# Attention in a two-layer hybrid backbone: one product for two heads' prompt logits, and the maxima's transposes one tile later

## The chip, the cores and the metric

The kernel runs on one core of a Trainium2 chip. The metric is the device time of one execution in microseconds (us); smaller is better. The core's engines work from queues of their own, in the order in which the program was laid out at compile time: TensorE (PE, with its weight loads as PEld), VectorE (DVE), ScalarE (ACT), GpSimd (POOL) and SyncE (SP), which here issues nearly all transfers.

## The reference, cut to what matters

Two layers run over 128 prompt tokens and 1024 latent tokens. In each layer attention (8 heads of 64, 2 key/value heads), a gated convolution and a long convolution run side by side on parts of one projection; their outputs are joined, projected and added, and a convolutional feed-forward part follows. Prompt tokens attend only to the prompt's own keys; latent tokens attend to their own keys and to 128 cached ones.

```python
def _blocked_attention(q, k, v):          # q (B, Lq, H, d); k, v (B, Lk, KV, d)
    ...
    def one_block(qi):
        s = jnp.einsum('bqkgd,bskd->bkgqs', qi, k, preferred_element_type=jnp.float32) * scale
        p = jax.nn.softmax(s, axis=-1).astype(v.dtype)
        return jnp.einsum('bkgqs,bskd->bqkgd', p, v)
    ...

def _layer(x, cond, p, pos, ctx_kv):
    ...
    if pos is None:                       # prompt
        keys, vals = k, v
    else:                                 # latents
        q, k = _rope_2d(q, rows, cols), _rope_2d(k, rows, cols)
        keys = jnp.concatenate([k, ctx_kv[0].astype(k.dtype)], axis=1)
        vals = jnp.concatenate([v, ctx_kv[1].astype(v.dtype)], axis=1)
    attn_out = _blocked_attention(q, keys, vals)
    ...
```

## The kernel before

Each layer has four phases: phase1 (norm, projection of the input, the long convolution, the norm and rotation of q and k), phase2 (attention, the gated convolution's taps, and products for the modulation vectors), phase3 (output projection) and phase4 (feed-forward). The order of the instructions in each engine's queue is laid out at compile time by a planner: it simulates the program with its own costs and gives each engine, whenever it is free in that simulation, the ready instruction with the highest priority. Priority is the program's order, shifted by named offsets: `soon()` moves what is inside 100 instructions ahead (OUT_PRIO), and the taps are moved 300 back (TAPS_PRIO), so that they fill VectorE's gaps.

The latents' attention works on head pairs j = 0 to 3, in two halves of 512 queries. `attention` (line 1375) has 4 x 2 x 9 = 72 loop steps a layer. A step makes the logits of one block of 128 keys for two heads (tile st, in a single buffer), has ScalarE take the exponentials (tile p), and multiplies earlier p by the values (tile av). In each step it also calls `next` on the generator `maxes` of the next head pair and on each side generator: the prompt's attention, the convolution (six taps a step, then its later parts), and the modulation. After the 40th step the side generators are called three times a step.

The softmax's maximum over the keys must be known before st is formed. `maxes` (line 1329) computes the logits a first time, in the other orientation: for each block (512 queries of one head) four tiles of 128 queries, each of three products S of 384 keys, each followed by a maximum on VectorE (tile mx, line 1357). S has three PSUM buffers. After the fourth tile three small steps on VectorE (lines 1363 to 1365) form the negated maximum as two parts (tile nmx); TensorE transposes them (tile mxt, in the same three buffers), and ScalarE copies them into two spare rows of the query tile (line 1347), so that the product for st subtracts the maximum. These transposes are queued behind tile MX_LAG of the next block (`put`, line 1343); for the first two blocks of a layer (MX_NOW) at once; for the last block of a head pair at the end of the generator, one loop step later.

`prompt_attention` (line 1286) treats one head pair in two loop steps. The first loads q, and for each of the two heads forms a product of 64 rows (tile sp), takes the maximum (pnb, line 1306), negates it (line 1307), and takes the exponentials with their sums (pp). The second step scales by the sums' reciprocals (line 1313), transposes (ppt), copies (ppm) and multiplies by the values (avp). All PSUM tiles of the side generators, and the row sums of the latents, share one bank (pool pa, one buffer): each of its users must wait until the last reader of the one before is done.

Of the kernel before, what the change touches and what calls it, by code (L numbers as in the profile page):

```python
# [9 lines left out]
F32 = mybir.dt.float32  # L10
F32R = mybir.dt.float32r
AF = mybir.ActivationFunctionType
ALU = mybir.AluOpType
AX = mybir.AxisListType
# [114 lines left out]

MX_LAG = 1  # L130

# [5 lines left out]
class Kern:  # L137
# [1148 lines left out]
    def prompt_attention(self, l, kp):  # L1286
        nc = self.nc
        KP = []
        for g in range(2):
            t = kp.tile([128, 128], F32, tag=f"kp{g}", name="kpt")  # L1290
            for u in range(2):
                nc.sync.dma_start(t[64 * u : 64 * u + 64, :], self.kpD[64 * g : 64 * g + 64, :])
            KP.append(t)
        VP = kp.tile([128, 128], F32, tag="vp", name="vpt")
        nc.sync.dma_start(VP[:], self.vpD[:])
        for j in range(4):
# [3 lines left out]
            rs = self.small([128, 2], "prs")  # L1300
            for hd in range(2):
                r = slice(64 * hd, 64 * hd + 64)
                t = self.T("sp")
                self.mm(t[:, :128], qp[r, :128], KP[g][r, :], True, True)
                nb = self.small([128, 1], "pnb")
                nc.vector.tensor_reduce(nb[:], t[:, :128], op=ALU.max, axis=AX.X)
                nc.vector.tensor_scalar(nb[:], nb[:], -1.0, None, op0=ALU.mult)
                self.act(P[:, 128 * hd : 128 * hd + 128], t[:, :128], AF.Exp, bias=nb[:], accum_out=rs[:, hd : hd + 1])
            nc.vector.reciprocal(rs[:], rs[:])
            yield  # L1310
            for hd in range(2):
                p = P[:, 128 * hd : 128 * hd + 128]
                nc.vector.tensor_scalar(p, p, rs[:, hd : hd + 1], None, op0=ALU.mult)
            t = self.T("ppt")
# [14 lines left out]
    def maxes(self, j):  # L1329
# [19 lines left out]
        for half in range(2):  # L1349
            for a, b in Q:  # L1350
                m3 = self.small([128, 4, 3], "mx3")
                for k in range(4):
# [8 lines left out]
                    if k == 3:  # L1361
                        mx, n = self.small([128, 4], "mx"), self.small([128, 4, 2], "nmx", F32R)
                        nc.vector.tensor_reduce(mx[:], m3[:], op=ALU.max, axis=AX.X)
                        nc.vector.tensor_scalar(n[:, :, 0], mx[:], -1.0, None, op0=ALU.mult)
                        self.stt(n[:, :, 1], mx[:], -1.0, n[:, :, 0].bitcast(F32), ALU.mult, ALU.subtract)
                        tail = b, half, n
                        if MX_NOW(j, half):
                            put(*tail)
                            tail = None
# [514 lines left out]
```

## Time and profile before

| | us |
|---|---|
| median of 3 runs | 3329.2 (3327.6 to 3332.85) |
| profiled execution: its own time | 3328.34 |
| its span, first to last instruction | 3326.3 |
| TensorE busy | 3126.4 (94%) |
| VectorE busy | 2167.1 (65%) |
| ScalarE busy | 1188.7 (36%) |
| GpSimd busy | 400.8 (12%) |

Busy time is the time in which an engine had an instruction in work; a share of it is an average over phases with different limits. The granted clock is that of TensorE, as a share of its full 2.4 GHz: 0.50 is the lower level of 1.2 GHz. A row of the timeline gives start and duration in us, then the engine, the source line, the operation, and out<-in by the names of the tiles; in brackets stands the time that the engine had been idle before it, and what released it. All times are from the first instruction of the span. Times on GpSimd and ends of matmuls are rough.

### The profile page before, as it was taken

Reading aid. Unit: us, or ns where it says so; the run is one execution under the profiler, and the core shown is the slowest. Engines: PE = TensorE matmul, PEld = TensorE weight load, DVE = VectorE, ACT = ScalarE, POOL = GpSimd, SP = SyncE. Lnnn points to the kernel's source line nnn. Section 1 sums busy time; section 2 is a strip of 40 time slices with the busy share of each in tenths; the row PEclk is TensorE's granted clock in tenths of the full one; section 3 lists DMA queues with packets and bytes.
Section 4 is the critical chain, followed back from the end, with each engine's and each line's share of the span. In section 5 each row is a group of like instructions: output and inputs, shape, how many; then the busy total and the mean of one; then the engine's idle time right before and its main releaser. Section 6 shows DMA issues by size and latency. Waiting matters only on the chain. (4 is left out here: it accounts for less than half of the span.)

```text
span 3326.3 us, 44636 instructions
## 1 busy us (share of the span) xinstructions
PE 3126.4 (94%) x17330; PEld 2763.4 (83%) x17330; DVE 2167.1 (65%) x3556; ACT 1188.7 (36%) x1964; POOL 400.8 (12%) x328
## 2 busy tenths in 40 slices
PE   5999788999799999999998997799999999999997
PEld 3899733459799999999998995345799999999997
DVE  6888799655765544555567897987265455555556
ACT  3433333452352223333344333335243333333223
POOL 5200034221210000000010003322110000000002
PEclk8899878999899999999999997899999999999998
DMA  7565535544311111111113546341511111111112
GB/s 282 168 235 176 172 133 171 175 164 140 127 39 43 43 42 42 43 44 42 42 57 134 167 143 207 111 159 65 187 30 47 42 45 42 42 42 45 42 42 70
DMA packets 152326, 336.08 MB, mean 101 GB/s; under 512 B 21359, under 2 KB 57843, under 8 KB 145588
## 3 DMA queue, kind: packets, MB, share of 16 engines
q1 hardware_dynamic: 147412, 318.69, 29.7%
q0 software_dynamic: 4704, 14.55, 1.5%
q8 instruction: 137, 2.24, 0.3%
q14 instruction: 73, 0.60, 0.1%
HBM read 264.86 MB, written 68.31 MB: 100 GB/s over the span
## 5 line engine op out<-in xcount | busy, mean ns | idle before, releaser
L241 PE MATMUL up<-hl,whi 128*128 128x384 f32 (+1 forms) x2112 | 712.6, 338 | 4.9 <-DVE hl L227 3.2
L241 PE MATMUL up<-hh,whi 128*128 128x384 f32 (+1 forms) x2112 | 709.8, 337 | 3.6 <-ACT hh L212 2.7
L241 PE MATMUL up<-hh,wlo 128*128 128x384 f32 (+1 forms) x2112 | 711.6, 337 | 0.0
L215 DVE TENSOR_TENSOR wlo<-wraw,whi 128x512 fp32r<-128x512 f32 x362 | 253.0, 699 | 646.9 <-ACT whi L235 646.5
L235 ACT CAST whi<-wraw 128x512 fp32r<-128x512 f32 x362 | 223.7, 618 | 876.2 <-PE dn L241 358.2
L241 PEld LDWEIGHTS up<-hl,whi 128*128 128x128 f32 x2112 | 398.7, 189 | 7.1 <-DVE hl L227 4.9
L241 PEld LDWEIGHTS up<-hh,whi 128*128 128x128 f32 x2112 | 398.1, 189 | 4.3 <-ACT hh L212 3.1
L241 PEld LDWEIGHTS up<-hh,wlo 128*128 128x128 f32 x2112 | 398.6, 189 | 0.0
L227 DVE SCALAR_TENSOR_TENSOR xt<-dn,mod,xt 128x128 f32<-128x128 f32 (+2 forms) x704 | 332.1, 512 | 71.4 <-PE dn L241 71.1
L241 PE MATMUL dn<-gh,wlo 128*128 128x384 f32 (+1 forms) x1056 | 359.0, 340 | 0.0
L241 PE MATMUL dn<-gh,whi 128*128 128x384 f32 (+1 forms) x1056 | 358.1, 339 | 0.0
L241 PE MATMUL dn<-gl,whi 128*128 128x384 f32 (+1 forms) x1056 | 357.4, 338 | 0.0
L227 DVE SCALAR_TENSOR_TENSOR fu<-pd,vec,fu 128x1154 f32<-128x1154 f32 (+2 forms) x192 | 253.9, 1323 | 91.7 <-ACT fu L212 89.2
L241 PE MATMUL win<-hl,whi 128*128 128x384 f32 x768 | 264.5, 344 | 5.2 <-DVE hl L227 5.1
L241 PE MATMUL win<-hh,wlo 128*128 128x384 f32 x768 | 262.4, 343 | 3.2 <-DVE wlo L215 3.2
L241 PE MATMUL win<-hh,whi 128*128 128x384 f32 x768 | 262.2, 345 | 2.8 <-ACT hh L212 1.1
L215 POOL TENSOR_TENSOR acc<-acc,sq 128x384 f32<-128x384 f32 x51 | 55.1, 1090 | 1635.6 <-ACT sq L212 1634.5
L1678 ACT COPY pd<-up 128x384 f32<-128x384 f32 (+1 forms) x352 | 131.8, 401 | 239.6 <-PE up L241 239.6
L1357 DVE TENSOR_REDUCE mx<-S 128x1 f32<-128x384 f32 x384 | 196.0, 546 | 28.2 <-PE S L241 27.3
L212 ACT ACTIVATE p<-st 128x1024 f32<-128x1024 f32 x144 | 147.1, 1022 | 162.8 <-PE st L241 162.2
L241 PEld LDWEIGHTS dn<-gl,whi 128*128 128x128 f32 x1056 | 199.9, 189 | 0.0
L241 PEld LDWEIGHTS dn<-gh,whi 128*128 128x128 f32 x1056 | 199.7, 189 | 0.0
(293 smaller groups left out, 5092.8 us busy)
## 6 DMA issues: line engine op xcount, KB each, us to landing
wmod<-in_w_mod SPq DMA_DIRECT2D x48, 1024.0 KB
wraw<-in_w_up SPq DMA_DIRECT2D x176, 256.0 KB
wraw<-in_w_dn SPq DMA_DIRECT2D x88, 256.0 KB
wraw<-in_w_in SPq DMA_DIRECT2D x64, 256.0 KB
q<-qD SPq DMA_DIRECT2D x48, 256.0 KB
mh<-mixD SPq DMA_DIRECT2D x16, 576.0 KB
ml<-mixD SPq DMA_DIRECT2D x16, 576.0 KB
khD<-fK SPq DMA_DIRECT2D x16, 512.0 KB
```

What stands on the lines that cost most here:

```text
L212: return self.nc.scalar.activation(out, in_, f, **k)
L215: return (eng or self.nc.vector).tensor_tensor(out, a, b, op=op)
L227: return (eng or self.nc.vector).scalar_tensor_tensor(out, a, s, b, op0=op0, op1=op1)
L235: self.nc.scalar.copy(hi, src)
L241: self.nc.tensor.matmul(out, l, r, start=start, stop=stop)
L1357: nc.vector.tensor_reduce(m3[:, k, s : s + 1], S[:, :384], op=ALU.max, axis=AX.X)
L1678: self.nc.scalar.copy(p[:, u + o : v + o], t[:, u - a : v - a])
```

## The change

The prompt's keys lie in a tile of 128 rows and two column blocks for each key head: the keys' 64 rows stand in the upper half of the first block and in the lower half of the second one, the other halves are set to zero by GpSimd. One product of 128 rows and 256 columns then gives the logits of both heads. One maximum over a 3-D view, one negation, two exponentials and the scaling follow it, all moved ahead by `soon()`. A head pair now takes four loop steps in place of two: load q; product and softmax; nothing; transposes and values. In `maxes` the transposes are queued one tile later (MX_LAG 2), and the three small steps that feed them are moved ahead by `soon()`.

```diff
@@ -127,7 +127,7 @@
 
 ORDER = [([10, 11, 12, 13, 14, 15, 0, 4, 5, 1, 8, 6, 9, 7, 2, 3], 9), ([10, 11, 12, 13, 14, 15, 0, 4, 5, 1, 8, 6, 9, 7, 2, 3], 9)]
 
-MX_LAG = 1
+MX_LAG = 2
 
 
 def MX_NOW(j, half):
@@ -1287,9 +1287,11 @@
         nc = self.nc
         KP = []
         for g in range(2):
-            t = kp.tile([128, 128], F32, tag=f"kp{g}", name="kpt")
+
+            t = kp.tile([128, 2, 128], F32, tag=f"kp{g}", name="kpt")
             for u in range(2):
-                nc.sync.dma_start(t[64 * u : 64 * u + 64, :], self.kpD[64 * g : 64 * g + 64, :])
+                nc.gpsimd.memset(t[64 * u : 64 * u + 64, 1 - u, :], 0.0)
+                nc.sync.dma_start(t[64 * u : 64 * u + 64, u, :], self.kpD[64 * g : 64 * g + 64, :])
             KP.append(t)
         VP = kp.tile([128, 128], F32, tag="vp", name="vpt")
         nc.sync.dma_start(VP[:], self.vpD[:])
@@ -1298,19 +1300,22 @@
             qp, P = self.M("qp"), self.M("pp")
             nc.sync.dma_start(qp[:, :128], self.qpD[j])
             rs = self.small([128, 2], "prs")
-            for hd in range(2):
-                r = slice(64 * hd, 64 * hd + 64)
-                t = self.T("sp")
-                self.mm(t[:, :128], qp[r, :128], KP[g][r, :], True, True)
-                nb = self.small([128, 1], "pnb")
-                nc.vector.tensor_reduce(nb[:], t[:, :128], op=ALU.max, axis=AX.X)
+
+            yield
+            t = self.T("sp")
+            self.mm(t[:, :256], qp[:, :128], KP[g][:].rearrange("p a b -> p (a b)"), True, True)
+            with self.soon():
+                nb = self.small([128, 2], "pnb")
+                nc.vector.tensor_reduce(nb[:], t[:, :256].rearrange("p (a b) -> p a b", a=2), op=ALU.max, axis=AX.X)
                 nc.vector.tensor_scalar(nb[:], nb[:], -1.0, None, op0=ALU.mult)
-                self.act(P[:, 128 * hd : 128 * hd + 128], t[:, :128], AF.Exp, bias=nb[:], accum_out=rs[:, hd : hd + 1])
-            nc.vector.reciprocal(rs[:], rs[:])
-            yield
-            for hd in range(2):
-                p = P[:, 128 * hd : 128 * hd + 128]
-                nc.vector.tensor_scalar(p, p, rs[:, hd : hd + 1], None, op0=ALU.mult)
+                for hd in range(2):
+                    self.act(P[:, 128 * hd : 128 * hd + 128], t[:, 128 * hd : 128 * hd + 128], AF.Exp, bias=nb[:, hd : hd + 1], accum_out=rs[:, hd : hd + 1])
+                nc.vector.reciprocal(rs[:], rs[:])
+                for hd in range(2):
+                    p = P[:, 128 * hd : 128 * hd + 128]
+                    nc.vector.tensor_scalar(p, p, rs[:, hd : hd + 1], None, op0=ALU.mult)
+            yield
+            yield
             t = self.T("ppt")
             for hd in range(2):
                 self.tr(t[:, 128 * hd : 128 * hd + 128], P[:, 128 * hd : 128 * hd + 128])
@@ -1360,9 +1365,10 @@
                         tail = None
                     if k == 3:
                         mx, n = self.small([128, 4], "mx"), self.small([128, 4, 2], "nmx", F32R)
-                        nc.vector.tensor_reduce(mx[:], m3[:], op=ALU.max, axis=AX.X)
-                        nc.vector.tensor_scalar(n[:, :, 0], mx[:], -1.0, None, op0=ALU.mult)
-                        self.stt(n[:, :, 1], mx[:], -1.0, n[:, :, 0].bitcast(F32), ALU.mult, ALU.subtract)
+                        with self.soon():
+                            nc.vector.tensor_reduce(mx[:], m3[:], op=ALU.max, axis=AX.X)
+                            nc.vector.tensor_scalar(n[:, :, 0], mx[:], -1.0, None, op0=ALU.mult)
+                            self.stt(n[:, :, 1], mx[:], -1.0, n[:, :, 0].bitcast(F32), ALU.mult, ALU.subtract)
                         tail = b, half, n
                         if MX_NOW(j, half):
                             put(*tail)
```

## Rows read from the trace of the kernel before

**Rows 1.** Page, part 1: busy us (share of the span) xinstructions

```profile
PE 3126.4 (94%) x17330; PEld 2763.4 (83%) x17330; DVE 2167.1 (65%) x3556; ACT 1188.7 (36%) x1964; POOL 400.8 (12%) x328
```

**Rows 2.** Stretches: window, length, busy PE, PEld, DVE, ACT, POOL; PEclk, DMA

```profile
411.00:580.00 169.00, 141.34 (x552) 64.08 (x551) 159.36 (x257) 61.05 (x87) 63.59 (x34) 0.82 0.46 155
580.00:740.00 160.00, 153.06 (x746) 75.76 (x745) 98.71 (x190) 77.75 (x105) 46.75 (x20) 0.99 0.47 159
2031.00:2205.00 174.00, 138.71 (x568) 65.34 (x566) 167.96 (x280) 64.91 (x96) 63.18 (x37) 0.84 0.47 155
2205.00:2356.00 151.00, 145.22 (x676) 73.32 (x675) 97.34 (x181) 76.87 (x104) 44.72 (x19) 1.00 0.37 122
```

**Rows 3.** PE's waits, 411 to 580: total us, times, longest us

```profile
PE S L241 <- DVE mx L1357: 7.8, 7, 2.3
PE mxt L251 <- DVE nmx L227: 7.8, 6, 2.6
```

**Rows 4.** PE's waits, 2031 to 2205

```profile
PE mxt L251 <- DVE nmx L227: 13.8, 6, 5.1
PE ppt L251 <- DVE pp L1313: 5.6, 2, 5.0
```

**Rows 5.** Timeline of PE: start, us, engine, line, operation, tiles [idle before <-releaser]

```profile
463.16 0.60 PE L251 MATMUL mxt<-cst,nmx 128*2 128x128 f32 x4 [0.80 <-DVE nmx L227]
...
479.06 0.79 PE L241 MATMUL sp<-kpt,qp 64*128 64x128 f32 x2 [5.87 <-ACT pp L212]
480.21 1.01 PE L251 MATMUL mxt<-cst,nmx 128*2 128x128 f32 x4 [0.35 <-DVE nmx L227]
...
2055.26 0.66 PE L251 MATMUL ppt<-cst,pp 128*128 128x128 f32 x2 [4.95 <-DVE pp L1313]
2057.48 1.01 PE L251 MATMUL mxt<-cst,nmx 128*2 128x128 f32 x4 [1.55 <-DVE nmx L227]
...
2153.56 1.01 PE L251 MATMUL mxt<-cst,nmx 128*2 128x128 f32 x4 [5.11 <-DVE nmx L227]
...
2312.01 0.60 PE L251 MATMUL mxt<-cst,nmx 128*2 128x128 f32 x4 [0.79 <-DVE mx L1357]
```

**Rows 6.** Timeline of DVE at the last of the three small steps

```profile
480.00 0.15 DVE L227 SCALAR_TENSOR_TENSOR nmx<-mx,nmx 128x4 fp32r<-128x4 f32 x1
...
2056.04 1.38 DVE L227 SCALAR_TENSOR_TENSOR nmx<-mx,nmx 128x4 fp32r<-128x4 f32 x1
```

**Rows 7.** DVE's groups, 411 to 580: busy us, mean ns | idle before

```profile
L1357 DVE TENSOR_REDUCE mx<-S 128x1 f32<-128x384 f32 x104 | 52.8, 546 | 5.9 <-PE S L241 5.6
```

**Rows 8.** DVE's groups, 2031 to 2205

```profile
L1357 DVE TENSOR_REDUCE mx<-S 128x1 f32<-128x384 f32 x106 | 54.1, 545 | 4.2 <-PE S L241 4.2
```

**Rows 9.** Tile pnb, whole span: ns min/median/max, first, last start us

```profile
L1306 DVE TENSOR_REDUCE pnb<-sp x16: 234/278/292, 398.3 to 2142.9; 128x1 f32<-128x128 f32 x16
L1307 DVE TENSOR_SCALAR pnb<-pnb x16: 136/141/151, 399.4 to 2146.3; 128x1 f32<-128x1 f32 x16
```

**Rows 10.** Timeline of all engines, start of layer 0's attention

```profile
400.19 1.28 ACT L212 ACT_TABLE_LOAD   x1
...
409.72 1.30 PE L241 MATMUL S<-k,q 128*128 128x384 f32 x3 [1.72 <-DMA q<-qD]
```

**Rows 11.** Timeline of PE, ends of both loops

```profile
711.55 0.33 PE L241 MATMUL pw<-cxh,wlo 128*128 128x384 f32 x1
...
731.84 1.20 PE L241 MATMUL st<-q,k 128*128 128x512 f32 x4
...
2323.59 0.33 PE L241 MATMUL pw<-cxh,wlo 128*128 128x384 f32 x1
...
2348.70 1.20 PE L241 MATMUL st<-q,k 128*128 128x512 f32 x4
```

**Rows 12.** Timeline of POOL, 380 to 440

```profile
388.36 0.21 POOL L1476 MEMSET cu<- 128x15 f32 x3 [0.48 <-issue]
429.43 11.40 POOL L215 TENSOR_TENSOR cz<-cz 128x584 f32<-128x584 f32 x6 [40.86 <-ACT cz L212]
```

## The prediction

> **What bounds the kernel now.** I read the page's first part, then the table of busy time by stretches for the two attention stages (one in each layer), then the matrix engine's waits in them, then single rows of the timeline at the places that the diff touches. TensorE is busy for 94% of the span [rows 1], so outside attention there is little to win, and the diff touches nothing there. The two attention stages last 329 us (411 to 740) and 325 us (2031 to 2356). Each falls into two stretches of a different kind [rows 2]. In the first the depthwise taps (tile ca) run on VectorE: DVE is busy for 159.4 of 169 us and 168.0 of 174 us, while PE is idle for 27.7 and 35.3 us and its granted clock is 0.82 and 0.84. In the second the taps are done: PE is busy for 153.1 of 160 us and 145.2 of 151 us at a clock of 0.99 and 1.00, and DVE is idle for over a third. So VectorE is the bound of the first stretches and TensorE that of the second ones. That decides what a removed wait is worth: in full in a second stretch; in a first one only what VectorE gains by it.
>
> The waits of PE in the first stretches that the change aims at [rows 3 to 5]: the second head's product waits for the first head's exponentials (5.9 us, one place); the prompt's transposes wait for the scaled weights (5.6 us, two places, one of 4.95); the transposes of the maxima wait for their negated copies (7.8 and 13.8 us). Of this last group only those that the code puts into the next block are moved by MX_LAG; the first two blocks of a layer are put at once and the last block of each head pair at the end. Of the 32 groups of these transposes eight are lagged ones in the first stretches, from 463.16 on; five of the eight waited, 0.80, 2.42, 0.30, 2.43 and 5.11 us (the first and the last stand in [rows 5]): 11.1 us. The other 10.5 us of the two sums stay where they are. So the change addresses 5.9 + 5.6 + 11.1 = 22.6 us of the 63.0 us of PE's idle time there, that is 36%.
>
> **The change part by part.**
> (1) One product for two heads. Per head pair VectorE loses one maximum (two of 278 ns over 128 columns become one over 256 columns) and one negation (141 ns) [rows 9]. The 256-column maximum has no row; between 278 ns for 128 and 546 ns for 384 columns [rows 7, 9] it lies at about 412 ns. 2 x 278 + 2 x 141 - 412 - 141 = 285 ns, and there are 8 pairs in the two layers: 2.3 us. They lie on the engine that bounds its stretch; if taps that could have waited fill the room it is 0. I take 2.3 (0 to 2.3). PE's two products become one of twice the columns; PE is not the bound there, so I count nothing. The exponentials keep their number. The four memsets a layer go to GpSimd, ahead of the tap buffers' own memsets (three of 128 x 15 take 0.21 us [rows 12]), and before its next work, at 429, that engine sits idle for 40.86 us [rows 12]; even ten times the row of the memsets is hidden by that, and a key tile that came too late would first be needed one loop step after the one in which it is needed now.
>
> What the first product's wait of 5.87 us is worth must be read from what comes next on PE. The transposes at 480.21 wait for a negated maximum that VectorE ends only at 480.15 [rows 5, 6]. Had the second product not waited, PE would have stood before the transposes until the same moment. The wait of 4.95 us at 2055.26 is the same: behind it PE stands until 2057.48 for a step that VectorE began at 2056.04 and that took 1.38 us [rows 5, 6]. Both of these transposes are of the kind that the new lag doesn't move. So the two largest waits of the prompt part are covered by the next wait, and are worth nothing by themselves as long as VectorE's order stays.
>
> The Trainium skill (TensorEngine Tiling, section Tiling Modes) has a rule against this part: products on different 64-row tiles of the array run in parallel, and padding to 128 rows gives that up. The trace shows no such overlap here: the second product waits for the first one's exponentials [rows 5], since both use the one PSUM bank of the side ring. By the rule the padded product would cost up to one more product of 0.79 us for each of the 8 pairs, 6.3 us, on an engine that has idle time there; the sum doesn't use it.
>
> (2) The extra steps. The product comes one loop step after its load of q, and the transposes two steps later than the product. At the start of layer 0 the softmax's first exponential makes ScalarE load a table (1.28 us at 400.19); casts of rotated q stand behind it in ScalarE's queue, SyncE issues the q loads behind the stores of those casts, and PE's first S product waited for q at 409.72, 1.72 us [rows 10]. With the product a step later the table load can fall behind that cast. Bounds: 0 and 1.3 us; I take 0.6.
>
> (3) The lag and the steps ahead. As VectorE bounds the first stretches, what the 22.6 us are worth is what VectorE itself lost by PE being late: its maxima waited 5.6 and 4.2 us for S products there [rows 7, 8], 9.8 us. I give the change its 36% of that: 3.5 us; ends 0 (another PE wait keeps S late: S already waits 7.8 us for the maxima's bank [rows 3], and three S products move ahead of the transposes into the same three banks) and 9.8. Queued behind each moved group are the copy of the maxima on ScalarE and the next S products; the copy is needed only when its head pair becomes the current one, so nobody waits for it sooner.
>
> (4) In the second stretches two lagged transposes waited, 0.38 us at 2243 and 0.79 us at 2312 (the second stands in [rows 5]): 1.2 us, on the bound engine, taken in full (0 to 1.2).
>
> Sum: 2.3 + 0.6 + 3.5 + 1.2 = 7.6 us. The profiled execution took 3328.34 us (span 3326.3, and 2.04 around it): 3320.7. The median of the three runs is 0.9 above the profiled execution, so the forecast is 3321.6; its own range, by the ends of the terms (0 to 14.6), is 3314.6 to 3329.2.
>
> **The rivals.**
> A. *The forecast*: VectorE lets only a part through. 3321.6.
>
> B. *The planner moves taps out of the first stretch.* Fewer stalls in its plan mean that fewer taps fit between the maxima, and VectorE has 61.3 and 53.7 us idle in the second stretches [rows 2] to take them. Then PE's addressed waits count in full: 22.6 + 1.2 = 23.8 us, 3305.4. For it: the taps have the lowest priority, and the convolution behind them ends 20 and 25 us before the last products of the loop [rows 11]. Against it: VectorE's order is fixed at compile time, and the two largest waits are covered by the next one.
>
> C. *The prompt's part, spread over 16 loop steps instead of 8, keeps the side bank from the convolution* (slower). Sums, convolution, modulation and prompt all take turns in one PSUM bank. The loop has 72 steps in 329 and 325 us, about 4.5 us each [rows 2], so the last pair may end up to 8 x 4.5 = 36 us later, and what is later in the turn, the convolution's products, with it. Its last product ends at 711.9 and 2323.9, the loop's last logits begin at 731.8 and 2348.7 [rows 11]: up to 20 us of delay cost nothing; beyond that the convolution becomes the end of the stage. At the full 36 us: 16 + 11 = 27 us; at 20 or less: 0. Where it happens I take the middle, 14 us: 3321.6 + 14 = 3335.6. Against it: the turns are not evenly tied to the loop, and the softmax steps go ahead, so each turn is shorter, and there are three turns a pair instead of four.
>
> D. *The small steps ahead don't come earlier, and the change does nothing.* The negated copy took 1.38 us at 2056.04 and 0.15 us at 480.00 [rows 6]; the long ones fall where GpSimd adds tap products. A step that is first in its queue and then held there is no earlier, taps go on filling the time between dependent steps, and S waits in place of the transposes. Then only the 2.3 us of removed work are left, or less: 3327. The Trainium skill (SBUF — State Buffer, section Who interferes with whom) says the same of the cause: such a VectorE step and a GpSimd operation that came first exclude each other for the whole of that operation. The rows of 1.38 us agree with it.
>
> **How the numbers follow.** A 0.47, B 0.15, C 0.22, D 0.16. A measurement of this kernel can tell about 0.2%, 6.7 us, from no change. A lies at 7.6, so it counts for 0.27 as faster and for 0.20 as the same; B is faster, D the same, C slower. Faster 0.27 + 0.15 = 0.42, same 0.20 + 0.16 = 0.36, slower 0.22. Predicted is the likeliest case, 3321.6. The range reaches down to B (3305) and up a little beyond C (3338): of B a half and of C some four tenths lie outside, 0.08 + 0.09.
>
> **What would show it.** Right: in the first stretches DVE's busy share stays at 95% or more, the waits of the lagged transposes fall below 2 us, the wait of S for the maxima grows by some of what they lose, and each stage becomes 2 to 6 us shorter. The prompt's part has four maxima and four negations a layer fewer. B would show taps after 590 and 2215 and a clock above 0.9 in the first stretches. C would show the last pw product within 5 us of the last st product, or behind it. D would show transposes that still wait 10 us or more in the two first stretches. The prediction is wrong if the time changes outside the two attention stages, or if the taps end at the same time while a stage loses more than 10 us.

## The result and the profile after

The change makes the kernel slower. Its ratio to the kernel before is 1.0051, with a 95% interval of 1.0036 to 1.0067: 17 us, 12 to 22. The undisturbed executions took 3340.45 to 3352.29 us (a fifth one, of 3661.97 us, was disturbed and is in no ratio) against 3327.6 to 3332.85. The median of all five is 3348.4; the forecast was 3321.6 and its range ended at 3338.

The profiled execution after has a span of 3346.6 us, 20.3 more than before. I split both spans at the same events. *Start* is the time from the start of the last product of the input projection (tile win) to the start of the first S product, *stage* from there to the start of the first product of the output projection (tile wo), *wo to up* from there to the first product of the feed-forward part (tile up), and *feed-forward* from the first to the last of those. All starts are read to 0.1 us.

| us | start 0 | stage 0 | start 1 | stage 1 | wo to up, layer 1 | feed-forward, layer 1 |
|---|---|---|---|---|---|---|
| before | 30.9 | 330.3 | 16.6 | 324.9 | 106.0 | 812.5 |
| after | 31.4 | 335.6 | 22.4 | 330.6 | 107.4 | 815.6 |

So 5.3 and 5.7 us came in the two stages, 5.8 us ahead of the second one, and 4.5 us behind it. The last 4.5 us follow no edit: in 40 us near the start of that feed-forward part (from 2480, before from 2463) the granted clock was 0.87 after and 0.96 before, and eight of the eighteen kernels below do not have them. I leave them aside.

**What the engines did.** The page's first part, then the stretches that answer to [rows 2] (same columns):

```profile
PE 3136.0 (94%) x17314; PEld 2766.8 (83%) x17314; DVE 2175.9 (65%) x3540; ACT 1188.1 (36%) x1964; POOL 402.0 (12%) x336
```

```profile
408.00:577.00 169.00, 142.73 (x548) 64.80 (x550) 157.00 (x251) 60.25 (x88) 63.83 (x33) 0.80 0.48 159
577.00:744.00 167.00, 156.59 (x753) 77.63 (x753) 107.91 (x191) 78.82 (x106) 46.76 (x20) 0.99 0.45 153
2041.00:2215.00 174.00, 139.85 (x561) 63.00 (x561) 163.37 (x266) 64.47 (x97) 65.31 (x37) 0.86 0.48 156
2215.00:2371.00 156.00, 147.35 (x670) 74.63 (x668) 104.25 (x187) 76.43 (x104) 43.53 (x19) 0.98 0.34 114
```

The first windows are as long as those of [rows 2], so a longer stage shows in the second ones: 167 and 156 us in place of 160 and 151. PE is idle there for 10.4 and 8.7 us in place of 6.9 and 5.8, so the loss does lie there. VectorE has 9 and 7 us more of work in them. In layer 1 four taps (5.0 us) are part of it; in layer 0 it is one tap, and for the most part the same steps taking longer. In the first stretches VectorE's share fell to 93 and 94%, below the 95% that I had asked for. Now PE's waits in the first stretch of layer 0 and then of layer 1, which answer to [rows 3, 4]:

```profile
PE S L241 <- DVE mx L1362: 9.4, 10, 2.5
PE mxt L251 <- DVE nmx L227: 6.2, 4, 2.6
PE modt L251 <- DVE modm L215: 3.0, 1, 3.0
...
PE S L241 <- DVE mx L1362: 9.9, 10, 2.7
PE mxt L251 <- DVE nmx L227: 6.8, 3, 4.0
PE modp L241 <- DMA wmod<-in_w_mod: 4.5, 1, 4.5
PE modp L241 <- DVE ml L215: 2.5, 1, 2.5
PE modt L251 <- DVE modm L215: 1.8, 1, 1.8
PE ppt L251 <- DVE modm L215: 1.5, 1, 1.5
```

The waits that the change aimed at did go. The transposes of the maxima wait for 6.8 instead of 13.8 us in layer 1. The eight lagged groups of the first stretches wait for 0.22 us in all, where they waited for 11.1. What is left belongs to groups that the lag does not move, like the one at 2201.53 (timeline of PE after, the one lagged group that still waits and the longest wait of the others):

```profile
531.51 0.86 PE L251 MATMUL mxt<-cst,nmx 128*2 128x128 f32 x4 [0.22 <-DVE mx L1362]
...
2201.53 1.01 PE L251 MATMUL mxt<-cst,nmx 128*2 128x128 f32 x4 [4.03 <-DVE nmx L227]
```

The wait of 5.87 us for the first head's exponentials has no row any more, the scaled weights none in layer 1. In their place stand others: S for the maxima's banks, and the modulation's products and transposes (modp, modt) and the prompt's transposes for the side bank, until VectorE has read it. The longest new one in layer 1, 4.5 us, is a modulation product that waits for its weights, at 2064. VectorE's maxima now wait longer for S, not less; in windows as long as those of [rows 7, 8] the group has

```profile
L1362 DVE TENSOR_REDUCE mx<-S 128x1 f32<-128x384 f32 x104 | 53.2, 547 | 9.4 <-PE S L241 9.3
...
L1362 DVE TENSOR_REDUCE mx<-S 128x1 f32<-128x384 f32 x103 | 52.3, 544 | 8.9 <-PE S L241 8.8
```

9.4 and 8.9 us where 5.9 and 4.2 stood.

**Where in a stage it went.** A stage lasts as long as PE's work at full clock, plus PE's idle time, plus what a lower clock costs. I summed idle time, and busy time x (1 - granted clock), over all windows of 2 us. In layer 0 the idle time rose from 34.6 to 36.4 us and the loss to the clock from 26.8 to 30.0: 5.0 of the 5.3 us. In layer 1 they rose from 41.0 to 42.8 and from 19.5 to 22.2: 4.5 of 5.7. More than half of these 9.5 us, 5.9, is the clock. Layer 1 in stretches of 60 us shows where, first before, then after:

```profile
2031.00:2091.00 60.00, 45.51 (x167) 23.25 (x166) 56.76 (x105) 24.43 (x38) 24.75 (x16) 0.75 0.54 170
2091.00:2151.00 60.00, 46.21 (x180) 20.37 (x178) 58.54 (x89) 23.03 (x36) 26.53 (x17) 0.84 0.44 139
2151.00:2211.00 60.00, 52.69 (x246) 24.54 (x248) 57.30 (x94) 20.24 (x26) 15.44 (x7) 0.93 0.46 163
2211.00:2271.00 60.00, 58.19 (x282) 29.98 (x280) 40.07 (x88) 27.80 (x37) 14.81 (x7) 1.00 0.33 94
2271.00:2355.90 84.90, 81.24 (x373) 40.41 (x369) 52.64 (x88) 46.29 (x65) 26.38 (x11) 1.00 0.38 133
```

```profile
2040.80:2100.80 60.00, 44.94 (x168) 21.96 (x166) 54.48 (x96) 20.97 (x33) 23.87 (x15) 0.75 0.64 207
2100.80:2160.80 60.00, 50.44 (x226) 21.21 (x224) 59.40 (x99) 23.80 (x40) 24.40 (x14) 0.97 0.62 207
2160.80:2220.80 60.00, 49.80 (x191) 22.29 (x190) 55.34 (x80) 22.30 (x29) 19.12 (x9) 0.89 0.13 43
2220.80:2280.80 60.00, 55.40 (x238) 29.01 (x237) 42.72 (x87) 21.91 (x28) 15.14 (x7) 0.94 0.36 110
2280.80:2371.40 90.60, 87.23 (x419) 43.73 (x417) 55.72 (x93) 51.92 (x74) 26.30 (x11) 1.00 0.34 122
```

The second 60 us carry the gain that was hoped for, and more: PE is busy for 50.4 instead of 46.2 us at a clock of 0.97 instead of 0.84. By the fine windows idle time and clock cost 11.3 us there instead of 20.9. The third and the fourth give it back: 16.4 instead of 10.3, and 7.8 instead of 1.8. Part of what the third lacks is work that was done earlier. Here are the modulation's products alone (tile modp) in the third 60 us, layer 1 and layer 0, before and after; they hang on no step of the attention and so can fill PE's gaps:

```profile
2151.00:2211.00 60.00, 7.90 (x64) 1.56 (x64) 2.03 (x3) 0.59 (x1) 0.93 0.46 163
529.70:589.70 60.00, 8.71 (x64) 1.67 (x64) 2.04 (x3) 0.58 (x1) 0.93 0.54 190
```

```profile
2160.80:2220.80 60.00, 1.92 (x16) 0.42 (x16) 0.68 (x1) 0.00 (x0) 0.89 0.13 43
528.30:588.30 60.00, 0.00 (x0) 0.00 (x0) 0.00 (x0) 0.00 (x0) 0.86 0.16 55
```

**The start of layer 1.** The timeline of GpSimd before; then that of GpSimd, VectorE and PE after:

```profile
2002.18 0.56 POOL L1253 DMA_DIRECT2D k<-kD  x1 [156.70 <-PE iy L241]
```

```profile
2018.60 0.91 POOL L1293 MEMSET kpt<- 64x128 f32 x4 [169.16 <-PE win L241]
2019.45 0.56 POOL L1253 DMA_DIRECT2D k<-kD  x1
...
2034.08 0.29 DVE L215 TENSOR_TENSOR ml<-hyo,mh 128x128 fp32r<-128x128 f32 x1 [9.22 <-DMA mixD<-ml]
...
2034.60 1.55 PE L241 MATMUL nr<-cst,nsd 128*64 128x128 f32 x12 [9.29 <-DVE nsd L1084]
...
2040.83 1.33 PE L241 MATMUL S<-k,q 128*128 128x384 f32 x3
```

The memsets wait until the last win product has read the memory that the padded key tile takes over. GpSimd also issues the loads of the latents' keys, and they stand behind the memsets in its queue: they go out at 2019.45, 17 us later than before (13 us, counted from the last win product). They now run at the same time as the stores of the long convolution's output, and take 8.6 us from issue to landing at the median instead of 5.0. VectorE stands 9.22 us for such a store (1.19 before), with the reciprocals for the rotated queries queued behind it, and PE 9.29 us behind those. In layer 0 the memsets come at 377.14 and the loads of the keys 2.2 us later than before; PE's first S product waits for q there in any case.

### The profile page after: what moved, and what is told of

The parts are those of the page before. It is cut to its first block, busy times and chain, and to the rows that moved or that the text cites. A ratio compares the mean times of both kernels' runs of the same rounds, so it can differ in the third digit from the quotient of the medians.

```text
span 3346.6 us, 44601 instructions
## 1 busy us (share of the span) xinstructions
PE 3136.0 (94%) x17314; PEld 2766.8 (83%) x17314; DVE 2175.9 (65%) x3540; ACT 1188.1 (36%) x1964; POOL 402.0 (12%) x336
## 4 chain that ended last, share of the span: by engine, by line
PE 76%; DVE 15%; DMA 5%; issue 1%; ACT 1%; SPq 1%; POOL 0%; DVEq 0%; ACTq 0%; POOLq 0%
PE up L241 32%; PE dn L241 16%; PE win L241 11%; PE wo L241 6%; DVE ca L227 4%; DVE mx L1362 2%; PE st L241 2%; PE av L241 2%; PE fc L241 1%; DVE nt L227 1%; PE S L241 1%; DMA orr<-sumr 1%; DVE hl L227 1%; DVE es L215 1%; PE flt L241 1%
## 5 line engine op out<-in xcount | busy, mean ns | idle before, releaser
L241 PEld LDWEIGHTS S<-k,q 128*128 128x128 f32 x384 | 76.0, 215 | 160.7 <-DVE mx L1362 66.4
```

The costliest lines, as they stand in the source:

```text
L241: self.nc.tensor.matmul(out, l, r, start=start, stop=stop)
```

## The experiments

All eighteen other kernels in one table; the ratios are to the kernel before (1.0010 is 3.3 us), the columns behind them are from each one's profiled execution.

| kernel | ratio, 95% interval | start 0 | stage 0 | start 1 | stage 1 |
|---|---|---|---|---|---|
| e1_maxima_only | 1.0033 [1.0022, 1.0044] | 31.1 | 335.4 | 17.0 | 331.7 |
| e2_prompt_only | 1.0024 [1.0014, 1.0035] | 30.7 | 330.8 | 20.0 | 327.5 |
| e3_keys_elsewhere | 1.0069 [1.0056, 1.0082] | 28.6 | 338.4 | 17.8 | 339.6 |
| e8_before_memsets | 1.0007 [0.9998, 1.0016] | 31.2 | 333.3 | 19.3 | 323.6 |
| e5_lag_only | 1.0032 [1.0020, 1.0044] | 31.7 | 334.6 | 17.2 | 330.1 |
| e6_ahead_only | 1.0000 [0.9990, 1.0009] | 30.7 | 332.4 | 16.5 | 325.1 |
| e9_steps_only | 1.0003 [0.9993, 1.0013] | 30.1 | 327.9 | 16.9 | 326.0 |
| e7_prompt_nosteps | 1.0024 [1.0015, 1.0033] | 27.5 | 332.5 | 17.7 | 326.1 |
| g1_product_alone | 1.0031 [1.0019, 1.0043] | 27.6 | 334.2 | 18.2 | 333.0 |
| f1_lag0 | 1.0067 [1.0053, 1.0081] | 31.1 | 342.5 | 16.6 | 333.3 |
| f2_lag3 | 1.0036 [1.0024, 1.0048] | 30.6 | 328.3 | 16.7 | 339.0 |
| f3_lag2_taps7 | 1.0037 [1.0025, 1.0050] | 30.3 | 338.7 | 17.1 | 331.9 |
| c1_taps7 | 1.0018 [1.0009, 1.0027] | 30.1 | 332.2 | 16.3 | 331.9 |
| d2_lag2_dvecast | 1.0032 [1.0021, 1.0043] | 30.4 | 333.6 | 17.0 | 325.8 |
| k1_after_dvezero | 1.0067 [1.0055, 1.0079] | 31.0 | 330.2 | 18.0 | 340.2 |
| i1_fewtaps | 0.9927 [0.9914, 0.9940] | 30.8 | 316.9 | 16.7 | 315.1 |
| i2_fewtaps_lag2 | 0.9933 [0.9919, 0.9948] | 30.4 | 320.4 | 16.2 | 321.8 |
| i3_fewtaps_change | 0.9935 [0.9921, 0.9948] | 31.0 | 317.1 | 22.0 | 313.7 |

How far one profiled execution can be trusted: e6_ahead_only, with the matrix engine's order unchanged and a ratio of 1.0000, differs from before by up to 2.1 us in a stage. Smaller differences of one stage are not read. Nor is the profiled execution the median one: e6's took 3334.2 us against a median of 3325.6, e7's 3329.4 against 3334.9. The ratios decide what a kernel costs; the stages only say where to look.

### Which part of the change

The two halves of the change, each alone; the memsets alone, on the kernel before; and the whole change with its key tiles zeroed elsewhere.

```diff
 e1:  MX_LAG = 1 -> 2, and self.soon() around the three small steps of mx
 e2:  all of prompt_attention as changed, MX_LAG = 1, no soon() in maxes
 e8:
-            t = kp.tile([128, 128], F32, tag=f"kp{g}", name="kpt")
+            t = kp.tile([128, 2, 128], F32, tag=f"kp{g}", name="kpt")
...
+                nc.gpsimd.memset(t[64 * u : 64 * u + 64, 1 - u, :], 0.0)
... (loads and the two products use the kept half of each block)
 e3 (on the change): the four memsets at the end of open_attention, tile from that pool
```

> Only the maxima's part: transposes one tile later and the three small steps ahead, the prompt as before. Theory 2a (this part makes the two stages longer, since VectorE serves its small steps ahead of maxima that S waits for): each stage 3 to 6 us longer than 330.3 and 325.0, 3335 to 3341. Rival 2b (the prompt's part makes them longer): stages as before or up to 5 us shorter, 3320 to 3330.

> Only the prompt's part: padded keys, one product, four steps a pair; lag 1 and the maxima's steps in their old place. Theory 1 with 2b: the late K loads (6 us) and longer stages (5 us each), 3342 to 3350. Theory 1 with 2a: the late K loads alone, 3333 to 3338. Theory of the prediction, rival C: the last convolution product within 5 us of the last st product.

> The kernel before with one addition: the prompt's key tile is twice as wide, its unused halves are set to zero by GpSimd, and the two products per pair read the same 64 rows as before. Theory 1 (the memsets stand ahead of the loads of K in GpSimd's queue and wait there for memory that the input projection holds, so that in layer 1 the loads start at about 2018 instead of 2002 and meet the stores of the long convolution): the first S product of layer 1 comes 5 to 10 us later than at 2031, the time is 3334 to 3340. Rival (the memsets are hidden as the prediction said, the loss lies in the changed order of the attention stages): 3327 to 3332, K loads' start no matter.

> The whole change, but the prompt's key tiles lie in the memory of the K tiles, and their memsets stand behind the loads of K on GpSimd. Theory 1: from the end of the input projection to the first S of layer 1 it takes 16 to 18 us again instead of 22.5, and 6 us of the 19 come back: 3340 to 3344 if the stages keep their loss. Rival (memsets don't matter): 3345 to 3352, and the distance stays at 22 us.

The maxima's half costs 11.0 us (7 to 15), the prompt's half 8.0 (5 to 12), together 19.0 against 17 for the whole: the halves add up. The memsets alone give 2.3 us (-0.7 to 5.3), which timing can't tell from nothing; start 1 grows by 2.7 us with them and by 3.4 and 5.8 us in e2 and in the change, and goes back to 17.8 when the tile lies elsewhere. That step is shown by the queue, by 2.7 us or more of start 1; its price in the whole kernel is not. But e3 does not win it back: its stages are 3 and 9 us longer than those of the change. Here moving one tile seems to have changed more than the start of the loads; what in the stages it was, no run shows.

### The lag, the small steps ahead, the extra steps, the product

```diff
 e5:  MX_LAG = 1 -> 2, nothing else
 e6:  self.soon() around the small steps of mx, nothing else
 e9:  two more yields in prompt_attention, nothing else
 e7:  one product, key tiles as in e3, no extra yields
 g1 (on e7):
-            with self.soon():
+            if True:
                 nb = self.small([128, 2], "pnb")
```

> The transposes of the maxima one block later, the small steps in their old place, nothing of the prompt's part. Theory 1 (the lag alone lengthens the stages: it changes the matrix engine's order, the small steps only the vector engine's): 3340, as with both together (3340.6), the taps again ending 183 and 190 us after the first S product (169.6 and 172.7 before) and each stage 5 to 7 us longer than 330.3 and 324.9. Theory 2 (the steps ahead are what delays the taps, since they take the place of taps in the vector engine's queue): 3329, the taps ending within 3 us of their old place.

> The small steps of the maxima ahead of taps, with the old lag of one block, nothing of the prompt's part. The order of the matrix engine is the same as before; only the vector engine's differs. Theory 1 (the lag alone is the loss): 3324 to 3329, since the transposes' waits of 11.1 us shrink and nothing else is moved. Theory 2 (the steps ahead are the loss): 3338 to 3341.

> The kernel before with the prompt's two extra steps alone: two products as before, key tiles as before, no memsets, small steps in their old place. It is also a second look at what a mere change of order does. Theory 1 (what the prompt's part loses beyond the memsets, about 5 us of its 7.7, comes from the new order of the work in the side bank): 3333 to 3335, the second stage 2 to 4 us longer, its taps ending 5 to 10 us later. Theory 2 (it comes from the product padded to 128 rows or from the small steps ahead): 3328 to 3330.

> The prompt's part without the two extra steps, the padded key tiles in the pool of the attention's keys (zeroed there, behind its loads): one product, small steps ahead. Theory 1 (the extra steps' order and the memsets ahead of the key loads are the loss): 3325 to 3329, start of layer 1 at 17 to 18 us, stages no longer than 330.3 and 324.9. Theory 2 (the padded product or the steps ahead are the loss): 3333 to 3335, the stages 2 to 4 us longer with the matrix engine later at the prompt's products.

> Of the prompt's part the one product alone: padded keys in the pool of the attention's keys, zeroed behind its loads; no extra steps, the small steps in their old place. With the small steps ahead as well it gave 3334.9 against 3326.5. Theory 1 (the small steps ahead cost nothing here either, as in the maxima's part; what costs is the product with its key tiles behind the q loads, which takes the first pair out of the idle time ahead of the first S product): 3332 to 3336, the first 60 us of a stage with 3 to 6 us more idle time of the matrix engine. Theory 2 (the small steps ahead are the loss): 3325 to 3329.

The lag alone costs 10.7 us, all of the maxima's half; its stages grow by 4.3 and 5.2 us. By the windows of 2 us the two layers lose it in different ways: in layer 1 PE's idle time falls from 41.0 to 36.8 us, as the lag was meant to do, and the loss to the clock rises from 19.5 to 27.2; in layer 0 the idle time rises from 34.6 to 38.9 and the loss to the clock falls from 26.8 to 24.1. The small steps ahead cost and give nothing (-3.3 to 3.0 us), although they were to shorten the transposes' waits. In the prompt's part neither the extra steps (1.0 us, -2.3 to 4.3) nor the small steps ahead (e7 and g1 overlap) are the loss; what is left in both is the product together with a key tile that lies and is zeroed elsewhere, 8 to 10 us. No run has the product alone with the tile in its place. From e2 (8.0), e8 (2.3) and e9 (1.0) I estimate 4.7 us for it and its small steps there, uncertain by some 5 us, and in e3 the other place was not free. The product itself is not dear for TensorE: its 16 instructions keep PE busy for 6.9 us in all, the 32 before for 9.9. In e7 and g1 the first pair falls out of the idle time ahead of the first S product (start 0 is 3.4 us shorter) and into the stage, as expected; that exchange is about even, so it isn't the loss.

### Does the lag cost by its size, or by where it leaves the taps?

I counted in VectorE's order behind which of the 192 maxima of a layer the last tap stands: 104 and 104 before, 116 and 123 with the lag of 2. The counts in the expectations were taken before the runs; in the traces they are the same, but for the lag of 0, 94 and 96, and the lag of 3, 112 and 102.

```diff
 f1:  MX_LAG = 1 -> 0
 f2:  MX_LAG = 1 -> 3
 f3:  MX_LAG = 1 -> 2 and P2_TAPS = 6 -> 7
```

> The kernel before with MX_LAG = 0 instead of 1 (the lag of 2 cost 10.7 us): the transposes follow the first three S products of the next block. In the vector engine's order the last tap of a layer then stands behind the 101st and the 108th of the 192 maxima over S products (before: 104 and 104; with lag 2: 116 and 123). Theory 1 (a lag costs by where it leaves the taps, since the convolution hangs on them): 3324 to 3332. Theory 2 (the lag costs by itself, more S products standing ahead of the transposes in three shared banks; so less lag is cheaper): 3319 to 3325, with shorter stages than before.

> The kernel before with MX_LAG = 3: twelve S products ahead of the transposes. The last tap stands behind the 103rd and the 101st of 192 maxima, as early as before. Theory 1 (where the taps end decides): 3322 to 3330, stages of 328 to 331 and 322 to 326 us, the last pair's nine blocks within 25 us and no fall of the clock in the last 60 us. Theory 2 (the lag by itself): 3340 or more, worse than the lag of 2 (3337.3).

> The lag of 2 alone, with the taps offered seven instead of six to a loop step. The last tap stands behind the 115th of the maxima in layer 0 (lag 2: 116), but behind the 107th in layer 1 (lag 2: 123). Theory 1: layer 1's stage is 324 to 327 us, as before, layer 0's 333 to 336 as with lag 2 alone; 3330 to 3333 in all. Theory 2 (the lag by itself): both stages as with lag 2 alone (334.6 and 330.1), 3336 to 3339.

Both theories fell. The lag of 0 costs 22 us although its last taps stand earlier than before, and with the lag of 3 layer 1 loses 14.1 us with the last tap at 102 while layer 0 loses nothing with it at 112. In f3 the last tap of layer 1 comes at 107 instead of 123, but its stage (331.9) is no shorter than with the lag of 2 alone, and the whole costs 12.3 us. So the place of the last tap doesn't order the times; and 0, 1, 2, 3 give 22, 0, 11 and 12 us, so the size of the lag doesn't either. The lag of 3 is the same edit in two layers with the same work: stage 0 is 328.3 us, stage 1 339.0.

### Any other order, one wait at the end, the memsets' queue

```diff
 c1 (on before):  P2_TAPS = 6 -> 7
 d2 (on e5; mix_out takes the engine of the cast as a new argument):
...
-        self.mix_out(l, j, O, 128 + 512 * half, 640 + 512 * half)
+        self.mix_out(l, j, O, 128 + 512 * half, 640 + 512 * half, nc.vector if j == 3 and half == 0 else "act")
 k1 (on the change):
-                nc.gpsimd.memset(t[64 * u : 64 * u + 64, 1 - u, :], 0.0)
+                nc.vector.memset(t[64 * u : 64 * u + 64, 1 - u, :], 0.0)
```

> A control: the kernel before, with the taps offered seven instead of six to a loop step and nothing of the change. The work is the same, the last tap stands behind the 106th of 192 maxima in both layers (before: 104), but the order of all five engines differs in many places. Theory N (any other order costs some 10 us, since the order of before is a good one among many, and lag and product cost only as other orders do): 3336 to 3342. Theory M (the parts of the change have mechanisms of their own, the order alone is worth a few us): 3325 to 3332.

> The lag of 2 alone, and the cast of the last but one output block of a layer (mh from av, fourth pair, first half), which stands in the scalar engine's queue ahead of exponentials while it waits for the sums' way through memory, moved to the vector engine. With the lag of 2 alone the matrix engine waited 3.5 us there in layer 1 and its clock then stood at 0.50 for 11 us. Theory E (a good half of what the lag costs in layer 1 is given back there): the wait of 3.5 us is gone, the clock at 1.00 to the end of the stage, stage 1 at 321 to 325 us instead of 330; 3329 to 3333 in all (lag 2 alone 3337). Rival (the loss is spread over the stage, this wait only covers another): 3336 to 3338.

> The whole change, with the four memsets of a layer on the vector engine instead of GpSimd, so that they no longer stand ahead of the key loads in GpSimd's queue. Theory Q (the queue costs 3 to 6 us at layer 1's start): start of layer 1 at 16 to 18 us instead of 22.4, 3342 to 3346 in all if the stages stay as they are. Rival (the vector engine's own queue, which carries the rotated queries, takes the wait instead): start at 20 us or more, 3348 or more. As the order of other work changes as well, the stages may move by some us either way; the start alone tells the theories apart.

The control costs 6.0 us (3 to 9), between what the two theories said. It is one sample: e6 and e9, which also change orders, cost 0.0 and 1.0. So about half of what the lag costs may need no mechanism of the lag's own; that is not shown. k1 shows the queue again, with start 1 back at 18.0 and the first load of the keys at 2003.11, and loses it in stage 1 (340.2), while its stage 0, with the same product and the same lag, is as short as before (330.2).

d2 belongs to the end of layer 1 with the lag of 2. There the convolution's last products lie between the last logits, and then PE stands (e5; timeline of PE, and between the dots rows of VectorE and ScalarE from the same window):

```profile
2340.60 1.08 PE L241 MATMUL av<-p,vt 128*64 128x512 f32 x4
2345.19 2.07 PE L241 MATMUL st<-q,k 128*128 128x512 f32 x4 [3.51 <-ACT p L212]
...
2342.87 0.69 DVE L215 TENSOR_TENSOR av<-av,orr 128x512 f32<-128x512 f32 x1 [3.47 <-DMA orr<-sumr]
...
2343.60 0.62 ACT L235 CAST mh<-av 128x512 fp32r<-128x512 f32 x1 [3.77 <-DVE av L215]
2344.12 1.02 ACT L212 ACTIVATE p<-st 128x1024 f32<-128x1024 f32 x1
```

ScalarE's next exponentials stand behind the cast of an output block, the cast behind VectorE's product, and that behind the row sums' way through memory. The windows around it show the clock (same columns as [rows 2]):

```profile
2340.00:2345.00 5.00, 1.68 (x7) 0.39 (x6) 2.13 (x3) 1.40 (x2) 0.00 (x0) 0.95 0.37 127
2345.00:2350.00 5.00, 4.81 (x10) 2.26 (x11) 2.00 (x3) 1.16 (x2) 2.71 (x1) 0.50 0.99 318
2350.00:2355.00 5.00, 5.00 (x13) 1.89 (x14) 0.00 (x0) 1.02 (x1) 2.35 (x1) 0.52 1.03 422
```

After the 3.5 us of idle time the clock is at its lower level, 1.2 GHz, for 10 us, which costs 4.81 x 0.50 + 5.00 x 0.48 = 4.8 us more. With the cast on VectorE (d2) the same windows show both gone,

```profile
2345.00:2350.00 5.00, 4.72 (x20) 1.74 (x16) 4.97 (x5) 2.45 (x3) 3.02 (x2) 1.00 0.59 206
2350.00:2355.00 5.00, 4.83 (x22) 1.65 (x20) 3.58 (x2) 1.58 (x2) 1.27 (x1) 1.00 1.02 337
```

but PE's timeline goes on with

```profile
2364.33 1.97 PE L241 MATMUL wo<-mh,whi 128*128 128x384 f32 x5 [4.66 <-DMA mh<-mixD]
```

The output projection now waits 4.66 us for the last output blocks on their way through memory, so the next chain takes up a part of the gain. Stage 1 is 4.3 us shorter than in e5, not the 5 to 9 expected. The ratio is the same 1.0032; with intervals of 4 us to either side it neither shows a gain of 4.3 us nor excludes it. So the chain is shown in the profile, and its worth in the kernel's time is not. In layer 0 of e5 that next one is there by itself, as in f3 (4.0 us); in the kernel before the first wo product waits for nothing there.

```profile
741.56 1.65 PE L241 MATMUL wo<-mh,whi 128*128 128x384 f32 x4 [3.52 <-DMA mh<-mixD]
```

### Without most of the taps

```diff
 i1 (on before), i2 (on e5), i3 (on the change):
-            for k in range(16):
+            for k in range(4):
                 with low():
                     s = h[:, 30:31] if k == 15 else ...
...
-            for k in range(15):
+            for k in range(4):
                 with low():
                     self.stt(y1, ...
```

> The kernel before with 46 of the 76 taps of a layer on the vector engine left out (its convolution is therefore not the reference's); the base for the two other kernels of this call, which are compared with it and not with the kernel before. 92 taps of some 0.8 us are 75 us of vector engine's time less: by what bounds the first stretches the stages should lose 20 to 35 us each, 3260 to 3290 in all.

> The same with a lag of 2. Theory T (a lag does harm through the taps: the order that it brings puts them in the matrix engine's way, and their convolution to the end of the stage): within 4 us of the same kernel with the lag of 1, rather below it. Rival (the lag does harm by itself, S products taking the shared banks ahead of transposes): 8 to 12 us above it, as with all taps (10.7).

> The same with the whole change. Theory T: 2 to 7 us above the kernel with few taps and no change: what is left is the memsets ahead of the key loads, start of layer 1 4 to 6 us longer, while the stages are within 3 us. Rival: 15 to 20 us above it, the stages 4 us or more longer each.

Leaving out 46 taps a layer (i1) saves 24 us in all, less than the 38 to 68 expected. With the 30 that stay the lag costs 0.0006 x 3328 = 2.0 us and the whole change 2.7, each about 6 us up or down by the two intervals; with all taps they cost 10.7 and 17. For the whole change that excludes the rival, and stages of 317.1 and 313.7 us against 316.9 and 315.1 say the same, with start 1 still 5.3 us longer. For the lag it doesn't quite: its profiled stages are 3.5 and 6.7 us longer, while the timed medians lie 1.5 us apart. So the whole change does its harm in the stages only with all the taps there; for the lag alone that is likely and not shown. How the taps bring it about is not shown either: with fewer taps VectorE is less full, but the convolution behind them also ends earlier, its last product beginning 41 us or more ahead of the last logits instead of 21 and 26. That what is moved finds no room on a full VectorE is my reading.

Of the kernels with all taps none is faster than the kernel before; e6, e8 and e9 can't be told from it.

## Why the prediction was wrong

The median lies 10 us above the range, and on the other side of no change.

1. **Part (1), the memsets "hidden" by 40.86 us of idle time.** Wrong. I looked at how long GpSimd was idle ahead of its next *computation* [rows 12], not at what else stands in its queue: the loads of the latents' keys. Nor did I ask what the memsets wait for: memory that the input projection still reads. The step costs 2.7 to 5.8 us at layer 1's start. The prediction's own sign, a change of time outside the two stages, caught it.

2. **Part (1), 2.3 us from VectorE's lost work.** The durations were right: the maximum over 256 columns takes 410 ns at the median (412 estimated), and the maxima and negations are 8 instead of 16 over the two layers. But no time follows: the prompt's half costs 8.0 us (5 to 12) where 2.3 were to be won, and the product with its tile elsewhere 10 (g1). The Trainium skill's rule that I set beside it (TensorEngine Tiling, section Tiling Modes: different 64-row tiles can run products in parallel, which I took padding to give up) does not explain the loss: the padded products keep PE busy for 6.9 us in all, the 64-row ones did for 9.9 us.

   Part (2), 0.6 us at the start of layer 0, can't be judged: start 0 is 31.4 us in place of 30.9, and 30.1 with the extra steps alone (e9), differences too small to be read from one profile.

3. **Part (3), 3.5 us of gain, with 0 as its lower end.** This is the step that decides. The lagged waits did go, as foretold (0.2 of 11.1 us are left), and VectorE's idle time for S was to shrink by its share; it grew from 5.9 and 4.2 to 9.4 and 8.9 us. Even that isn't a price by itself, since e6 has 8.9 us in layer 0 and is no slower. The bound was wrong in kind: I had no reason that excluded a loss, only the thought that a removed wait can do no worse than be replaced. The lag alone costs 10.7 us (7 to 15) in place of winning 3.5. The small steps ahead, which I priced together with the lag, are worth nothing.

4. **Part (4), 1.2 us in the second stretches.** Wrong in sign. They are where the stages lose: 167 and 156 us instead of 160 and 151. I counted their waits for the transposes and not what else would come into them. In layer 1 that is in part taps, the idea of rival B; in layer 0, with one tap, it is not.

5. **What the whole rested on: VectorE bounds the first stretches.** Only partly. Leaving out 46 taps a layer, some 38 us of VectorE's time by the 0.82 us of a tap, shortened the stages by 13.4 and 9.8 us. The stages won a third and a quarter of that time. I read that as PE, with its idle time and its lower clock, standing close behind.

6. **The rivals.** B's first sign came in layer 1 alone: the last tap begins 187.8 us after the first S product there (172.7 before), in layer 0 171.0 us after it (169.6). Its second did not: the clock was 0.97 for 60 us of layer 1, but 0.80 and 0.86 over the first stretches. Its price has the wrong sign: the gain of 9.6 us there is real, and 12 us are given back in the 120 us that follow. C named a place where the lag alone loses, the end of the stage behind the convolution, but by the wrong cause. In the change the last pw product begins 21 and 23 us ahead of the last st product (21 and 26 before, between the last single products of the groups in [rows 11]), and the extra steps cost 1.0 us; it is the lag alone that brings the convolution to the end (7.9 us ahead in layer 0). D is excluded by the lagged transposes, which hardly wait any more (0.22 us). The sum of all groups, 13.0 us, is still above D's 10, but nearly all of it is the 10.5 us and more of those that the lag does not move. Of its reason one part stands, that a small step first in its queue can still be held: a negation of the prompt's maxima took up to 2.3 us (154 ns at the median), with a step of GpSimd running from before it to its end.

What stays open: why a given order costs what it costs. The lag of 2 was followed to two chains at the ends of its stages, and the change to the work that was taken from the third 60 us. But e9 takes the modulation's products ahead in the same way, 64 in the second 60 us of layer 1 and 16 in the third, and costs 1.0 us. So that is where the time shows, not a cause that was isolated. Nor was it settled why the one product with its tile costs 8 to 10 us when the parts that were tried alone cost next to nothing. By the control some 6 us of either may be a matter of a new order.

## What to carry to other kernels

Where a planner lays out the order, an edit that moves a few instructions is a new order for all of them. Time a few changes of the order that leave the work as it is first; here three cost 0.0, 1.0 and 6.0 us, the last nearly as much as the gain of 7.6 us that was forecast. No term below that should be given a sign. Before an instruction is called hidden, read what stands behind it in its queue, DMA issues too, and what its memory waits for. And, as I read these runs, in a stretch where two engines are both nearly full a removed wait is worth only what the later stretches can spare: ask which work filled the gap until now, and what will be missing where it came from.

## What was not expected of the hardware

One wait of 3.5 us near the end of a stage cost more through the clock than by itself: 10 us at the lower level behind it, 4.8 us. In the last 90 us of the stages before, the lower clock cost 0.2 and 0.0 us. The padded product is the cheaper one for TensorE, 6.9 us busy against 9.9 us in all; the two 64-row products of a pair never ran beside each other, the second beginning 2.7 us or more after the first had ended.
